# Delta solver of a hybrid encoder block: scratch by direction and head, loads by ranges of rows, side transfers on Pool's queue

## Chip, cores and metric

One core of one Trainium2 chip runs the kernel. The metric is device time in microseconds of one execution; before, the median of three runs is 1564.22 us. A core has TensorE (PE, matmuls), VectorE (DVE), ScalarE (ACT), GpSimd (POOL) and SyncE (SP); transfers are issued by an engine's queue and carried by 16 shared DMA engines.

## The reference, cut to what matters

One layer of an encoder over 256 tokens and 2048 channels, and a final norm. The first projection feeds a gated delta mixer in both directions (8 heads of 128 channels, chunks of 64 tokens) and a dilated window attention; the output projection and a convolutional gated feed-forward follow. The change touches the triangular solve of the delta mixer:

```python
    a_mat = jnp.where(strict, jnp.einsum("bhnik,bhnjk->bhnij", k_beta, k) * gamma, 0.0)
    t_mat = a_mat + jnp.eye(c, dtype=jnp.float32)
    u = lax.linalg.triangular_solve(t_mat, v * beta[..., None], left_side=True,
                                    lower=True, unit_diagonal=True)
    w = lax.linalg.triangular_solve(t_mat, k_beta * jnp.exp(cum_g)[..., None], left_side=True,
                                    lower=True, unit_diagonal=True)
```

There are 8 heads x 4 chunks x 2 directions = 64 triangular matrices of 64 x 64. The kernel inverts them once and multiplies by the inverse.

## The kernel before

**Main stream.** All projections are one list of items. An item is half of a 1 MB weight block (a slab of 1024 rows by 256 columns, one of two column halves): ACT rounds it to float32r (`hi`, line 262), DVE makes the rest (`lo`, line 263), and TensorE multiplies both with the transposed input `xcat` (lines 313 and 316). Weight blocks go round four buffers (`raws`, NR = 4). `refill` (line 248) issues the next block on SP as soon as, in program order, the block four earlier has been split; on the chip SP waits at that instruction for the split to be done. Items are split LA = 3 ahead of their matmuls.

**Side work.** Everything else is written as generators. `pump` advances them by a step after each item within a budget of vector and scalar time, so the order of instructions on each engine is fixed when the program is built, and each engine follows its own order, held only by data and by the reuse of tiles.

**Delta mixer, first part.** For each head, `g_conv` convolves q, k and v into a record; `g_gates` writes the cumulated decays to `cg_d` and loads them back for all partitions into `gam` (line 584, one load for each head on SP), where POOL adds the mask (line 592) and ACT takes the exponential (line 601). `g_gram` (line 733) makes the strictly triangular blocks `at` (the reversed direction with reversed columns) and writes them to the DRAM scratch `a_d` (line 774, POOL), the record to `rec_d`; gates of the output go to `z_d`.

**Solver.** `g_solve` (line 823) starts when all of these are written. Its tiles W (the inverses), tm (products) and Bt (the matrices) reuse the memory of the first part. Partitions are problems: `dir*64 + (s^dir)*32 + q*8 + h`, where s is the column parity of the inverse; so each matrix lies in two partitions. Bt is loaded in three ranges of rows (0 to 8 by SP, 8 to 24 and 24 to 64 by POOL), 16 loads each, of 8 partitions a load (line 850). Then 63 steps j run between the items, two DVE instructions each (lines 858 and 859): row j of Bt times column j of W, added to W. ACT reverses the backward half into tm (line 864), and 32 transfers write the inverses to `u_d` (line 874, half on SP and half on POOL; heads 0 and 1 first).

**Recurrence.** `g_steps` (line 923) takes over the solver's memory: zz and oo lie where W was, UB1 mostly where tm was, rr and UB0 where Bt was. DVE clears UB0 and POOL clears UB1 (line 938). SP copies four small scales, loads the inverses of the first two heads into UB0 (`load_u`, line 944), the records into rr (`load_r`, line 951), and, after WAIT_FIRST = 8 steps of the pump, the next pair's inverses and the gates zz (line 972). Four steps for each pair of heads follow, with the matmul by the inverse at line 998. `g_tail` norms and gates the outputs; POOL takes a power in it (line 894).

Of the kernel before, what the change touches and what calls it, by code (L numbers as in the profile page):

```python
# [4 lines left out]
F32 = mybir.dt.float32  # L5
# [24 lines left out]
WAIT_SOLVE = 6  # L30
TWO_PI = 2.0 * np.pi

# columns of the constant array
# [49 lines left out]
def block_kernel(tc, A, out, dbg=None):  # L83
# [17 lines left out]
    def aview(t, off, dims):  # L101
        """A view of an SBUF or PSUM tile with free dims given as [step, count]."""
        return bass.AP(tensor=t.tensor, offset=t.offset + off, ap=[list(t.ap[0])] + [list(d) for d in dims])
# [7 lines left out]
    # ------------------------------------------------------------ persistent tiles  # L111
# [39 lines left out]
    a_d = dram.tile([H, 4, P, 64], F32, name="a_d")  # L151
    u_d = dram.tile([H, 2, 4, 64, 64], F32, name="u_d")
    h_d = dram.tile([T, D], F32, name="h_d")

    # ------------------------------------------------------------ side work
# [9 lines left out]
    def pump(bv, ba=None):  # L165
        """Advance each piece of side work by one step, within the vector and scalar engines' time."""
        ba = bv if ba is None else ba
        state["v"] = min(state["v"] + bv, bv)
        state["a"] = min(state["a"] + ba, ba)
        for t in list(gens):  # L170
            if state["v"] <= 0 or state["a"] <= 0:
                break
            while True:
                try:
                    c = next(t[2])
                except StopIteration:
                    gens.remove(t)
                    break
                more = False
                if not isinstance(c, tuple):  # L180
                    c = (c, 0)
                elif len(c) == 3:
                    more = True
                state["v"] -= c[0]
                state["a"] -= c[1]
                if not more or state["v"] <= 0:
                    break
# [42 lines left out]
    # ------------------------------------------------------------ main stream  # L230
# [36 lines left out]
    def run_items(upto=None):  # L267
        """Emit the matmuls of all items listed so far."""
# [31 lines left out]
    def cm_block(ch, j, done, width=P):  # L300
        """Channel-major product of one block of columns: acc = [w.T xh + wl.T xh | w.T xl]."""
# [27 lines left out]
    def evac(out_ap, acc, n=P, perm=None):  # L329
        """out = acc[:, :256] + acc[:, 256:]."""  # L330
# [9 lines left out]
    def natural(ap):  # L340
        """Destination in token order for a source in class order."""
        return ap.rearrange("p (m c) -> p c m", c=4)

    # ------------------------------------------------------------ loads of constants, first norm
# [4 lines left out]
    # the small weights pass through the tiles that later hold the rotary tables  # L349
# [17 lines left out]
    # list of the first projection's items  # L367
# [7 lines left out]
    def v_slab(c0, done):  # L375
        """Token-major product of 256 columns, in class order of the tokens."""
# [41 lines left out]
    # sums of squares, scaled rows, transposes; the gate columns' product follows the transposes  # L418
# [68 lines left out]
    # ------------------------------------------------------------ side: small weights, gates, rotary tables  # L487
# [19 lines left out]
    def ab_write(fn, dst, src):  # L507
        """Chunk order 0,3,2,1 of the 64-token chunks."""
# [4 lines left out]
    def g_gates(graw, gg_, gpool):  # L513
# [18 lines left out]
        # sigmoid(x) = exp(min(x, 0)) / (1 + exp(-|x|))  # L532
# [3 lines left out]
        # log1p(e) = 2 z (1 + z^2/3 + z^4/5 + ...), z = e / (2 + e)  # L536
# [17 lines left out]
        # slot q: (tile, orientation) = (A,FB) (B,FB) (B,BF) (A,BF)  # L554
# [27 lines left out]
        # decay matrices of all heads: exp(cg_i - cg_j) inside the triangles  # L582
        for h in range(H):
            nc.sync.dma_start(gam[h], bass.AP(tensor=cg_d.tensor, offset=cg_d.offset + h * 512, ap=[[0, P], [1, 512]]))
# [3 lines left out]
        # ex: 0 -cg, 1 exp(cg), 2 -exp(cg), 3 exp(tot-cg), 4 exp(total of lower), 5 exp(total of upper), 6 cg  # L588
# [21 lines left out]
    # ------------------------------------------------------------ delta heads: convolution, Gram blocks  # L610
# [9 lines left out]
    for t in recs.free:  # L620
        for hf in range(2):
            # the blocks of different chunks
            G.memset(aview(t[hf * 64 : hf * 64 + 64], 1024 + hf * 64, [[P, 4], [1, 64]]), 0.0)
# [6 lines left out]
    # more buffers for the convolutions, gone before the attention's  # L630
# [12 lines left out]
    # a record holds, per tile of two chunks, the columns k0 q0 q1 k1 (64 each), then k by tokens, v by tokens, and the  # L643
    # products of q and k with the tokens of q in the order 1, 0 of the chunks
    def qk_write(fn, r, c0, src):
        """Tile 0 has the chunks 0 and 3, tile 1 the chunks 2 and 1."""
# [20 lines left out]
    def g_conv(which, h, pad):  # L667
# [37 lines left out]
        if which < 2:  # L705
# [10 lines left out]
            if which == 1:  # L716
                # 2: sqrt(ss + eps), 3: 1 / (ss + eps)
                G.tensor_tensor(ss[:, 2, :, h : h + 1], sc, poshalf[:, 0:2].rearrange("p (x o) -> p x o", o=1), op=ALU.pow)
                V.reciprocal(ss[:, 3, :, h : h + 1], sc)
            else:  # L720
                # 4: (128 (ss + eps))^(-1/2)
# [11 lines left out]
    def g_gram(h):  # L733
# [4 lines left out]
        # 0: beta / (ss+eps) per slot, 1: -that, 2: that * exp(tot - cg)  # L738
# [8 lines left out]
        # rows 0-63: k0 with k0 q0, rows 64-127: k1 with q1 k1  # L747
# [26 lines left out]
        nc.gpsimd.dma_start(a_d[h].rearrange("q p c -> p q c"), at)  # L774
# [29 lines left out]
    def z_pads():  # L804
        """From here on no pad of the extra pool is handed out."""
# [9 lines left out]
    # ------------------------------------------------------------ delta: triangular inverses and recurrence  # L815
    mx = {}

    def natural_31(fn, dst, src):
        """Token order for a source in chunk order 3,0,1,2."""
# [3 lines left out]
    def g_solve():  # L823
# [10 lines left out]
        # partition = dir*64 + (s^dir)*32 + q*8 + h, columns 2m+s of the inverse; bwd problems with rows and columns reversed  # L834
# [3 lines left out]
        for r0, r1 in ((0, 8), (8, 24), (24, 64)):  # L838
            for d in range(2):
                for s in range(2):  # L840
                    for o in range(2):
                        hf = o ^ d
                        p0 = d * 64 + (s ^ d) * 32 + o * 16
                        for i in range(2):
                            q = o * 2 + i
                            # the reversed rows leave out the columns below the diagonal; the others come in one piece
                            row, sj, c0 = (63 - r0, -64, r0) if d else (r0, 64, 0)
                            base = a_d.offset + (q * P + hf * 64 + row) * 64 + c0
                            src = bass.AP(tensor=a_d.tensor, offset=base, ap=[[4 * P * 64, 8], [sj, r1 - r0], [1, 64 - c0]])
                            (nc.gpsimd if r0 else nc.sync).dma_start(Bt[p0 + i * 8 : p0 + i * 8 + 8, r0:r1, c0:], src)  # L850
        for _ in range(WAIT_SOLVE):
            yield 0
        for j in range(63):
            m, r = j // 2 + 1, 63 - j
# [10 lines left out]
        for h0, h1 in ((0, 2), (2, H)):  # L865
            for d in range(2):
                for s in range(2):
                    for q in range(4):
                        hf = (q // 2) ^ d
                        p0 = d * 64 + (s ^ d) * 32 + q * 8  # L870
                        src = W[p0 + h0 : p0 + h1] if d == 0 else wr[p0 + h0 : p0 + h1]
                        dst = bass.AP(tensor=u_d.tensor, offset=u_d.offset + ((h0 * 2 + hf) * 4 + q) * 4096 + (s ^ d) * 64,
                                      ap=[[8 * 4096, h1 - h0], [128, 32], [1, 64]])
                        (nc.sync if q % 2 else nc.gpsimd).dma_start(dst, src)
# [5 lines left out]
    def g_tail(g0, o_t, z_t, jk):  # L880
        """Gated RMS norm of the heads from g0 on."""
# [41 lines left out]
    def g_steps():  # L923
        gt, tp = pool("steps", side="left")
        NG = 2
        # what is needed first lies where the solver's last transfers do not read
# [13 lines left out]
        def load_u(g0):  # L940
            t = UB[(g0 // NG) % 2]
            for hf in range(2):
                for e in range(NG):
                    nc.sync.dma_start(t[hf * 64 : hf * 64 + 64, e, :, hf * 64 : hf * 64 + 64],
                                        u_d[g0 + e, hf].rearrange("q c r -> c q r"))

        def load_r(g0, part):
            if g0 < H:
                cs = (slice(0, 1024), slice(1024, 1536))[part]
                for e in range(NG):  # L950
                    nc.sync.dma_start(rr[e][:, cs], rec_d[g0 + e, :, cs])

        # the outputs' tokens are held in the order 1, 0 of the chunks of a tile, and so are their scales
# [9 lines left out]
        for g0 in range(0, H, NG):  # L963
# [7 lines left out]
            for e in range(NG):  # L971
                nc.sync.dma_start(z_t[e], z_d[g0 + e])
# [84 lines left out]
    # ------------------------------------------------------------ dilated attention  # L1057
# [9 lines left out]
    def g_tables():  # L1067
        # rotary tables: angle = pos * inv_freq, reduced to [-pi, pi] with exact products
# [43 lines left out]
    def v_hook(g, pr, acc):  # L1112
        # wait for the readers of the former pair
# [94 lines left out]
    # ------------------------------------------------------------ output projection items  # L1208
    go, op = None, None

    def tm_group(w, k0, nk, c0, acc_of, act, first, last, done):
        """Token-major product of k-tiles k0.. with 512 columns."""
# [91 lines left out]
    # ------------------------------------------------------------ feed-forward items  # L1304
    # the first columns take the first half of the rows of all four blocks before the second half
# [22 lines left out]
    # the last rows of the last columns: the first 128 tokens, then the others  # L1328
# [87 lines left out]
    # ------------------------------------------------------------ down projection, final norm  # L1416
# [72 lines left out]
```

## Time and profile before

| | |
|---|---|
| times of three runs, us | 1560.75, 1564.22, 1568.68 |
| span of the profiled execution, us | 1562.7 |
| TensorE busy | 1523.4 us, 97% |
| VectorE, ScalarE, GpSimd busy | 71%, 54%, 8% |
| DMA moved | 300.63 MB, 192 GB/s over the span |

The profile is of one execution, from the first instruction to the last; its span is 1.5 us under the median of the runs. Busy time of TensorE is that of pipelined matmuls, whose ends are modelled. A granted clock below 1 means that TensorE ran, for part of the stretch, at the lower of its two levels. [...]

### The profile page before, as it was taken

How to read it: one execution, taken by the hardware profiler on the slowest of the kernel's cores; microseconds unless marked ns; L12 is line 12 of the kernel's file. 1: busy time of each engine (PE TensorE's matmuls, PEld its weight loads, DVE VectorE, ACT ScalarE, POOL GpSimd, SP SyncE). 2: the span in 40 equal slices, each digit the busy share in tenths (PEclk: the TensorE clock that was granted, in tenths of full speed). 3: DMA queues.
4: the chain of work that ended last, by engine and by line, in shares of the span. 5: the costliest groups of instructions: out<-in, count | busy, mean ns of one | idle time of the engine just before them, and what ended most of it. 6: DMA issues, size and time to landing. Idle time of an engine off the chain costs nothing.

```text
span 1562.7 us, 23126 instructions
## 1 busy us (share of the span) xinstructions
PE 1523.4 (97%) x8827; PEld 1326.9 (85%) x8827; DVE 1102.3 (71%) x1872; ACT 847.5 (54%) x1518; POOL 132.5 (8%) x189
## 2 busy tenths in 40 slices
PE   7999999899998999999999999999999999999997
PEld 6878888798997898899788888888888888888886
DVE  5878986879864676776557777777777777455453
ACT  5588774555544555654446555555555555344342
POOL 3153344000020000000000000000000000000000
PEclk9999999899999999999999999999999999999999
DMA  9656789755658645655665565656555556666652
GB/s 254 216 173 222 220 265 186 223 163 161 191 147 227 199 136 164 207 162 175 216 216 194 170 206 172 197 181 194 184 186 191 184 193 231 202 210 212 196 188 81
DMA packets 253569, 300.63 MB, mean 192 GB/s; under 512 B 16645, under 2 KB 214454, under 8 KB 253010
## 3 DMA queue, kind: packets, MB, share of 16 engines
q1 hardware_dynamic: 246802, 279.51, 57.6%
q0 software_dynamic: 6224, 19.05, 4.3%
q8 instruction: 69, 1.13, 0.3%
q10 hardware_dynamic: 432, 0.59, 0.1%
q14 instruction: 42, 0.34, 0.1%
HBM read 285.41 MB, written 13.65 MB: 191 GB/s over the span
## 4 chain that ended last, share of the span: by engine, by line
PE 92%; DMA 3%; issue 1%; ACT 1%; DVE 1%; POOL 0%; SPq 0%; POOLq 0%; ACTq 0%; DVEq 0%
PE bank L313 38%; PE bank L316 19%; PE bank L1224 7%; PE bank L1226 7%; PE bank L1225 7%; PE bank L391 3%; PE bank L392 3%; PE bank L393 3%; DMA raw<-in_w_in_dram 3%; PE bank L982 1%; PE bank L1028 1%; PE bank L1023 1%; DMA xt<-in_x_dram 0%; PE bank L1198 0%; PE bank L1179 0%
## 5 line engine op out<-in xcount | busy, mean ns | idle before, releaser
L313 PE MATMUL bank<-xcat,hi 128*128 128x512 f32 x2688 | 952.2, 399 | 18.6 <-DVE qk L338 15.2
L263 DVE TENSOR_TENSOR lo<-raw,hi 128x1024 fp32r<-128x1024 f32 x504 | 619.0, 1229 | 361.0 <-ACT hi L262 357.2
L262 ACT ACTIVATE hi<-raw 128x1024 fp32r<-128x1024 f32 x504 | 533.0, 1059 | 546.0 <-PE bank L313 211.6
L316 PE MATMUL bank<-xcat,lo 128*128 128x256 f32 x2688 | 730.1, 282 | 0.0
L313 PEld LDWEIGHTS bank<-xcat,hi 128*128 128x128 f32 x2688 | 499.0, 189 | 126.9 <-DVE qk L338 16.3
L316 PEld LDWEIGHTS bank<-xcat,lo 128*128 128x128 f32 x2688 | 506.8, 189 | 13.4
L1224 PE MATMUL bank<-hi,gth 128*128 128x512 f32 x336 | 130.7, 389 | 0.0
L1226 PE MATMUL bank<-hi,gtl 128*128 128x512 f32 x336 | 130.7, 389 | 0.0
L1225 PE MATMUL bank<-lo,gth 128*128 128x512 f32 x336 | 130.7, 389 | 0.0
L391 PE MATMUL bank<-hi,xcat 128*128 128x256 f32 x384 | 108.6, 283 | 0.0
L393 PE MATMUL bank<-hi,xcat 128*128 128x256 f32 x384 | 106.5, 277 | 0.0
L392 PE MATMUL bank<-lo,xcat 128*128 128x256 f32 x384 | 106.4, 277 | 0.0
L1392 DVE SCALAR_TENSOR_TENSOR fy<-fpad,cwf,fy 128x256 f32<-128x256 f32 x176 | 84.8, 482 | 3.1
L1225 PEld LDWEIGHTS bank<-lo,gth 128*128 128x128 f32 x336 | 63.1, 188 | 13.2
L1226 PEld LDWEIGHTS bank<-hi,gtl 128*128 128x128 f32 x336 | 63.1, 188 | 13.1
L1224 PEld LDWEIGHTS bank<-hi,gth 128*128 128x128 f32 x336 | 63.1, 188 | 12.9
L391 PEld LDWEIGHTS bank<-hi,xcat 128*128 128x128 f32 x384 | 72.1, 188 | 0.5
L393 PEld LDWEIGHTS bank<-hi,xcat 128*128 128x128 f32 x384 | 72.4, 189 | 0.0
L392 PEld LDWEIGHTS bank<-lo,xcat 128*128 128x128 f32 x384 | 72.2, 188 | 0.1
L1224 PE MATMUL bank<-hi,mxh 128*128 128x512 f32 x128 | 51.4, 401 | 0.3 <-DVE hs L1262 0.3
L1226 PE MATMUL bank<-hi,mxl 128*128 128x512 f32 x128 | 50.6, 395 | 0.0
L1225 PE MATMUL bank<-lo,mxh 128*128 128x512 f32 x128 | 50.6, 395 | 0.0
(288 smaller groups left out, 1333.6 us busy)
## 6 DMA issues: line engine op xcount, KB each, us to landing
raw<-in_w_in_dram SPq DMA_DIRECT2D x104, 1024.0 KB
raw<-in_w_ffn_in_dram SPq DMA_DIRECT2D x88, 1024.0 KB
raw<-in_w_ffn_out_dram SPq DMA_DIRECT2D x44, 1024.0 KB
raw<-in_w_out_dram SPq DMA_DIRECT2D x14, 1024.0 KB
rec_d<-rec POOLq DMA_DIRECT2D x8, 768.0 KB, 5.3
rr<-rec_d SPq DMA_DIRECT2D x8, 512.0 KB
xt<-in_x_dram SPq DMA_DIRECT2D x4, 512.0 KB
gam<-cg_d SPq DMA_DIRECT2D x8, 256.0 KB
```

Of the source, the lines that this page charges most:

```text
L262: ACT(hi, src, AF.Copy)
L263: V.tensor_sub(lo, src, hi.bitcast(F32))
L313: mm(acc[:, :512], lhsT=hi[:, kk, :], rhs=xcat[:, k, :], start=k == 0, stop=k == KT - 1)
L316: mm(acc[:, :T], lhsT=lo[:, kk, :], rhs=xcat[:, k, :T], start=False, stop=False)
L391: mm(o, lhsT=xh, rhs=hi[:, kk, :], start=k == 0 and t == 0, stop=False, skip_group_check=True)
L392: mm(o, lhsT=xh, rhs=lo[:, kk, :], start=False, stop=False, skip_group_check=True)
L393: mm(o, lhsT=xl, rhs=hi[:, kk, :], start=False, stop=k == KT - 1, skip_group_check=True)
L982: mm(p1[:, e * T + hf * P : e * T + (hf + 1) * P], lhsT=rr[e][:, X * T + hf * P : X * T + (hf + 1) * P], rhs=SS[e][:, o ^ hf, :], start=Tr ...
L1224: mm(a[t], lhsT=xh, rhs=hi[:, kk, :], start=st, stop=False)
L1225: mm(a[t], lhsT=xh, rhs=lo[:, kk, :], start=False, stop=False)
L1226: mm(a[t], lhsT=xl, rhs=hi[:, kk, :], start=False, stop=sp_)
L1392: stt(y, pad[:, d : d + T], cwf[:, d, b : b + 1], y, op0=ALU.mult, op1=ALU.add)
```

## The change

Both scratch tensors are laid out by direction, head, chunk: `a_d` and `u_d` are `[2, H, 4, 64, 64]`. `g_gram` writes a head's blocks with four transfers in place of one. Bt gets the partition order `dir*64 + copy*32 + h*4 + q`, so that a load covers 64 partitions (forward; the source is read twice by a step of zero) or 32 (backward, whole rows, in reversed order). The rows come in four ranges; the loads of the last two stand at steps j = 6 and j = 16 of the solver's loop. All of Bt's loads are on POOL. The inverses are written with 8 transfers in place of 32, all on POOL. `load_u` uses eight transfers for a pair of heads in place of four. The loads of gam, UB, zz and, from the second pair of heads on, rr move from SP to POOL. Comments are left out of the file. The core of the diff:

```diff
+ROWS = ((0, 8), (8, 24), (24, 44), (44, 64))
...
-    a_d = dram.tile([H, 4, P, 64], F32, name="a_d")
-    u_d = dram.tile([H, 2, 4, 64, 64], F32, name="u_d")
+    a_d = dram.tile([2, H, 4, 64, 64], F32, name="a_d")
+    u_d = dram.tile([2, H, 4, 64, 64], F32, name="u_d")
...
-            nc.sync.dma_start(gam[h], bass.AP(tensor=cg_d.tensor, offset=cg_d.offset + h * 512, ap=[[0, P], [1, 512]]))
+            nc.gpsimd.dma_start(gam[h], bass.AP(tensor=cg_d.tensor, offset=cg_d.offset + h * 512, ap=[[0, P], [1, 512]]))
...
-        nc.gpsimd.dma_start(a_d[h].rearrange("q p c -> p q c"), at)
+
+        for o in range(2):
+            for hf in range(2):
+                d = o ^ hf
+                base = a_d.offset + ((d * H + h) * 4 + 2 * o) * 4096
+                dst = bass.AP(tensor=a_d.tensor, offset=base, ap=[[64, 64], [4096, 2], [1, 64]])
+                nc.gpsimd.dma_start(dst, at[hf * 64 : hf * 64 + 64, 2 * o : 2 * o + 2, :])
...
-        for r0, r1 in ((0, 8), (8, 24), (24, 64)):
-            for d in range(2):
-                for s in range(2):
-                    for o in range(2):
-                        hf = o ^ d
-                        p0 = d * 64 + (s ^ d) * 32 + o * 16
-                        for i in range(2):
-                            q = o * 2 + i
-                            # the reversed rows leave out the columns below the diagonal; the others come in one piece
-                            row, sj, c0 = (63 - r0, -64, r0) if d else (r0, 64, 0)
-                            base = a_d.offset + (q * P + hf * 64 + row) * 64 + c0
-                            src = bass.AP(tensor=a_d.tensor, offset=base, ap=[[4 * P * 64, 8], [sj, r1 - r0], [1, 64 - c0]])
-                            (nc.gpsimd if r0 else nc.sync).dma_start(Bt[p0 + i * 8 : p0 + i * 8 + 8, r0:r1, c0:], src)
+
+        def load_rows(r0, r1):
+            src = bass.AP(tensor=a_d.tensor, offset=a_d.offset + r0 * 64, ap=[[0, 2], [4096, 32], [1, (r1 - r0) * 64]])
+            nc.gpsimd.dma_start(Bt[0:64, r0:r1, :].rearrange("p r c -> p (r c)"), src)
+            for s in range(2):
+                src = bass.AP(tensor=a_d.tensor, offset=a_d.offset + 32 * 4096 + (63 - r0) * 64,
+                              ap=[[4096, 32], [-64, r1 - r0], [1, 64]])
+                nc.gpsimd.dma_start(Bt[64 + s * 32 : 96 + s * 32, r0:r1, :], src)
+
+        for r0, r1 in ROWS[:2]:
+            load_rows(r0, r1)
         for _ in range(WAIT_SOLVE):
             yield 0
         for j in range(63):
+            for r0, r1 in ROWS[2:]:
+                if j == r0 // 2 - 6:
+                    load_rows(r0, r1)
...
-                    for q in range(4):
-                        hf = (q // 2) ^ d
-                        p0 = d * 64 + (s ^ d) * 32 + q * 8
-                        src = W[p0 + h0 : p0 + h1] if d == 0 else wr[p0 + h0 : p0 + h1]
-                        dst = bass.AP(tensor=u_d.tensor, offset=u_d.offset + ((h0 * 2 + hf) * 4 + q) * 4096 + (s ^ d) * 64,
-                                      ap=[[8 * 4096, h1 - h0], [128, 32], [1, 64]])
-                        (nc.sync if q % 2 else nc.gpsimd).dma_start(dst, src)
+                    p0 = d * 64 + s * 32
+                    src = (wr if d else W)[p0 + h0 * 4 : p0 + h1 * 4]
+                    dst = bass.AP(tensor=u_d.tensor, offset=u_d.offset + (d * H + h0) * 4 * 4096 + s * 64,
+                                  ap=[[4096, (h1 - h0) * 4], [128, 32], [1, 64]])
+                    nc.gpsimd.dma_start(dst, src)
...
-                    nc.sync.dma_start(t[hf * 64 : hf * 64 + 64, e, :, hf * 64 : hf * 64 + 64],
-                                        u_d[g0 + e, hf].rearrange("q c r -> c q r"))
+                    for o in range(2):
+                        src = u_d[o ^ hf, g0 + e, 2 * o : 2 * o + 2].rearrange("q c r -> c q r")
+                        nc.gpsimd.dma_start(t[hf * 64 : hf * 64 + 64, e, 2 * o : 2 * o + 2, hf * 64 : hf * 64 + 64], src)
...
-                    nc.sync.dma_start(rr[e][:, cs], rec_d[g0 + e, :, cs])
-
-        # the outputs' tokens are held in the order 1, 0 of the chunks of a tile, and so are their scales
+                    (nc.gpsimd if g0 else nc.sync).dma_start(rr[e][:, cs], rec_d[g0 + e, :, cs])
...
-                nc.sync.dma_start(z_t[e], z_d[g0 + e])
+                nc.gpsimd.dma_start(z_t[e], z_d[g0 + e])
```

## Rows read from the trace of the kernel before

**Rows 1.** The page: span, and busy time with instruction count of two engines.

```profile
span 1562.7 us, 23126 instructions
...
PE 1523.4 (97%) x8827; PEld 1326.9 (85%) x8827; DVE 1102.3 (71%) x1872; ACT 847.5 (54%) x1518; POOL 132.5 (8%) x189
```

**Rows 2.** TensorE's instructions in order of time (start, duration; idle before and releaser).

```profile
280.31 0.79 PE L313 MATMUL bank<-xcat,hi 128*128 128x512 f32 x1 [7.42 <-DVE qk L338]
...
489.84 0.70 PE L998 MATMUL bank<-rr,UB 128*128 128x128 f32 x4
497.44 0.80 PE L313 MATMUL bank<-xcat,hi 128*128 128x512 f32 x1 [6.90 <-DVE qk L338]
```

**Rows 3.** Windows: stretch, busy time by engine, granted clock, DMA share, GB/s.

```profile
280.30:286.30 6.00, 5.99 (x19) 5.15 (x20) 5.53 (x9) 1.48 (x3) 0.00 (x0) 0.53 0.67 203
286.30:292.30 6.00, 6.00 (x36) 5.23 (x35) 5.45 (x10) 4.08 (x8) 0.00 (x0) 1.00 0.68 217
...
497.40:501.40 4.00, 3.96 (x13) 3.44 (x14) 3.93 (x7) 2.98 (x8) 0.00 (x0) 0.56 0.82 219
```

**Rows 4.** The chain of waits that ended last: start, duration, what.

```profile
251.46 26.04 DMA raw<-in_w_in_dram
...
836.03 0.47 PE bank L313 x2
841.64 0.47 PE bank L313 x2
```

**Rows 5.** SP's queue in order of time: start, duration from first to last issue.

```profile
63.95 5.18 SPq L584 DMA_DIRECT2D gam<-cg_d  x8
...
227.45 2.37 SPq L253 DMA_DIRECT2D raw<-in_w_in_dram  x2
236.64 5.99 SPq L850 DMA_DIRECT2D Bt<-a_d  x16
...
451.50 3.15 SPq L253 DMA_DIRECT2D raw<-in_w_in_dram  x2
455.89 2.96 SPq L874 DMA_DIRECT2D u_d<-W  x4
461.87 1.64 SPq L874 DMA_DIRECT2D u_d<-tm  x4
...
474.81 0.83 SPq L253 DMA_DIRECT2D raw<-in_w_in_dram  x1
...
483.90 2.82 SPq L951 DMA_DIRECT2D rr<-rec_d  x4
```

**Rows 6.** DMA queues from 243 to 275, then 275 to 280: packets, MB, share.

```profile
q1 hardware_dynamic: 4194, 4.11, 81.2%
q0 software_dynamic: 865, 1.28, 29.5%
...
q1 hardware_dynamic: 1714, 1.73, 108.0%
```

**Rows 7.** POOL's instructions in order of time around both ends of the solver.

```profile
236.99 10.54 POOL L850 DMA_DIRECT2D Bt<-a_d  x19 [2.59 <-issue]
...
456.46 0.67 POOL L874 DMA_DIRECT2D u_d<-W  x1 [190.41 <-DVE W L859]
...
464.74 2.68 POOL L874 DMA_DIRECT2D u_d<-W  x4
...
478.00 0.96 POOL L938 MEMSET UB<- 128x1024 f32 x1 [7.55 <-DMA u_d<-tm]
```

**Rows 8.** ACT's instructions in order of time: the first reader of gam there.

```profile
82.46 1.27 ACT L601 ACTIVATE gam<-gam,ex 128x128 f32<-128x128 f32 x4
```

**Rows 9.** DMA issues: queue, count, KB each, median us to landing.

```profile
u_d<-W POOLq DMA_DIRECT2D x4, 48.0 KB, 7.2
...
u_d<-W POOLq DMA_DIRECT2D x4, 16.0 KB, 3.3
```

## The prediction

> **What bounds the kernel now.** I read the page first: TensorE is busy for 1523.4 of 1562.7 us [rows 1], so the kernel is a stream of matmuls, and only idle or slowed time of that engine can be won. The order of its instructions in time shows two long holes in the middle: 7.42 us ahead of 280.31, and 6.90 us ahead of 497.44 [rows 2]. The windows behind each hole show a second loss: the granted clock is 0.53 for 6 us (19 matmuls, against 36 in the next 6 us at 1.00) and 0.56 for 4 us [rows 3]. This is the 1.2 GHz level after an idle spell, then 2.4 GHz again. At full clock the same work takes (1 - 0.53) x 6.0 = 2.8 us and (1 - 0.56) x 4.0 = 1.8 us less. So the first hole costs 7.4 + 2.8 = 10.2 us, the second 6.9 + 1.8 = 8.7 us, together 18.9 us. The rest of the idle time, some 25 us of 39, lies at the start, at the end and in small pieces, where the diff has nothing, or work off the chain.
>
> Why the holes are there: the chain of waits names the landing of a weight block. One raw block of 1 MB feeds two items, and the stream eats one in 5.6 us (841.64 - 836.03) [rows 4]. The block issued at 251.46 took 26.04 us to land [rows 4], and TensorE stood for 7.42 of them; so 18.6 us from issue to landing would have cost nothing. That is the slack of four raw buffers and of the items split ahead.
>
> The timeline of SP's queue says why the blocks were late. Before the first hole SP issued two raw blocks by 229.8, then none until 242.6: it stood in the solver's sixteen first loads (236.64 for 5.99 us, and ahead of them a wait for its tile's former use) [rows 5]. Before the second hole it issued none from 454.65 to 474.81, held by the sixteen writes of the inverse (from 455.89 on), one at 474.81, and then scales, UB and rr until 486.72 [rows 5]. That is 20.2 us, 3.6 blocks' worth, and then 11 us more.
>
> There is a second cause for the first hole: the blocks that were issued moved slowly. From 243 to 275 SP's queue moved 4.11 MB in 81.2% of 16 engines (101 engine-ns per KB), while Pool's Bt loads moved 1.28 MB in 29.5% (118 per KB); from 275 to 280, alone, SP's queue took 50 per KB [rows 6]. Something in the Bt loads made every packet take twice as long. They go to 8 partitions at a time, which I suspect, but no row separates that from the many short pieces.
>
> **The change, part by part.**
>
> *SP loses the Bt loads, the u_d writes, UB, later rr, z and gam.* In the two places that count, SP keeps only the four small copies of scales and the four rr loads of the first pair (2.82 us) [rows 5]. Nothing that SP keeps there waits for the solver's writes: rr lies where Bt was, which no write reads. Raw blocks are then issued as buffers come free. For the second hole that alone is worth 8.7 us. For the first it returns the 13 us between 229.8 and 242.6, more than two blocks, against a lateness of 7.4 us. So both holes should close if the transfers themselves don't get worse.
>
> *The Bt loads.* 48 loads become 12: per range of rows one for the forward half (64 partitions, one long run each) and two of 32 partitions for the reversed half, now whole rows of 256 bytes. The bytes grow from 1.8 to 2.1 MB, the short pieces stay at about 4100 but each is longer. The last two ranges are placed at the solver's steps 6 and 16, but this moves only their place in Pool's order: Pool has no instruction between the Bt loads and the first u_d write at 456.46 (idle 190.41 us before it) [rows 7], and the loads read nothing that the steps write. So I expect all twelve right after one another, from about 237. At the 118 engine-ns per KB of before, 2.1 MB are 247 engine-us, 15.5 us of all sixteen. Raw blocks need 50 x 1024 ns = 51 engine-us each, 3.2 of every 5.6 us. Bounds: if raw packets keep their 50 ns, nothing is lost; if all of the 15.5 us goes ahead of a raw block, it lands 15.5 + 3.2 = 18.7 us after issue, which is just the slack of 18.6; if the packets slow to 101 ns as before for 32 us, the deficit of before returns without SP's 13 us. I take 0, since two of the three bounds lie there; the other end is the whole 10.2 us.
>
> The Trainium skill (DMA: Bandwidth & Descriptors, Rules for kernel authors) says that an access whose outermost dimension has few counts, such as a leading zero-step broadcast, confines a transfer to that many engines. The forward loads now have such a source (zero step, count two); By that rule the sum would be between 18.9 us (each load on engines of its own) and 7.4 us (all on the same two); no load of before has such a source, so its trace neither agrees nor disagrees.
>
> *The a_d writes.* Eight become 32, 24 more issues on Pool at about 0.55 us (the mean of the nineteen Bt issues, 10.54 us) [rows 7]: 13 us more on an engine that is busy for 8% [rows 1], before the solver, spread over eight heads. Cost 0; with the cover gone (the last head's four writes ahead of the first Bt load) the loads start 1.6 us later.
>
> *The gam loads* go from SP (5.18 us of its queue [rows 5]) to Pool. They now stand on Pool behind a wait for the landing of cg_d, and Pool's small powers and the mask additions stand behind them. ACT's first use of gam is at 82.46 [rows 8], 13 us after SP had issued the last load (69.1); eight issues at 0.55 us are 4.4 us. I take 0; the bounds are 0 and some 2 us.
>
> *The u_d writes and UB.* 32 writes become 8, of 64 and 192 KB; all on Pool. 16 UB loads become 32, eight for each pair of heads. Here Pool's order matters. Behind the eight writes stands the memset of the second UB tile, which lies in tm and waits for the writes that read it; before, it ran at 478.00 after 7.55 us of idling [rows 7]. Behind the memset now stand the first eight UB loads, which SP issued before, and for them waits TensorE's first step (L998, 489.84 [rows 2]), with the whole matmul stream behind it. When do the writes land? Low: the last is issued at about 467 (461.9, when tm is copied [rows 5], and six issues of, by my estimate from the 0.67 us of one before, up to 0.9 us) and lands after the 7.2 us of a 48 KB write [rows 9], at 474. Middle: the same 4096 pieces as before, done as before at 478. High: Pool's queue wrote its half of the large pieces from 464.7 [rows 7] to about 477.5, 13 us for 1536; at that rate its 3584 pieces after 461.9 take 30 us, until 492. From there 0.96 us memset, eight issues at 0.67 and the 3.3 us landing of a small write [rows 9] are 9.7 us. UB is there at 484, 488 or 502, against 489.84. Cost 0, 0 or 11.9 + 1.8 for the clock = 13.7 us. I take the middle, 0, with 2 us to spare. (Times are those of before; all behind 280 moves 10 us forward together.)
>
> *rr and z of later pairs* go to Pool and wait there for their last readers, as they did on SP; behind them on Pool stand only the power of the gated norm and the next loads, which have a pair's time, some 50 us. Cost 0.
>
> **Sum.** The span loses 10.2 + 8.7 = 18.9: 1543.8. The median of the runs shown, 1564.22, is 1.5 us above the span; so 1545.3 for the time.
>
> **The rivals.**
> 1. *Both holes close*: 1545.3. Its own range is 1542 to 1549, for pieces of 1 to 3 us left over and the spread of runs.
> 2. *TensorE waits for UB in place of the second hole.* For it: Pool alone now issues writes, memset and loads in one order, and there are 2 us to spare. Against: larger writes over more partitions may go faster. Halfway between middle and high (485), UB lands at 494.7: 4.9 + 1.8 = 6.7, so 1552; at the high end 1559.
> 3. *The first hole stays, by the forward loads.* Their source steps twice over the same 32 blocks, so it has an outermost count of two. If they rest on two engines each, and on the same two, an engine that moves 1.73 MB / 5 us / 16 = 21.6 KB per us [rows 6] has 512 KB of them, 24.3 us, and 64 KB of a raw block, 3.0 us: 27.3 us to landing, 8.7 over the slack, and 2.8 for the clock, 11.5 in all: 1556.8. On different pairs, the largest load is 160 KB, 7.6 + 3.0 us, and nothing is lost. Before's slowness returning in full gives nearly the same, 1555.5.
> 4. *It does not do what it says*: the shared transfer engines, not SP's order, starve the stream in both places: 1564.
> 5. *Slower.* One mechanism at one place: raw blocks, which were held back while the inverse was written, now run beside the writes and halve Pool's rate. 3584 pieces take 60 us, until 522; UB lands at 531.7, TensorE stands for 41.9 us and 1.8: 1545.3 + 43.7 = 1589. It decides from where that wait passes 17 us, that is when the writes end after 497. Against it: between 462 and 478 the engines were far from full.
>
> **How the numbers follow.** Chances: 0.60, 0.14, 0.12, 0.07 and 0.07. I predict the first, 1545. For the range, the low end is the first rival's with some spread, 1541; the high end takes in the second and third with their upper bounds, 1560, and leaves the last two out. About 0.5%, 7.8 us, is what a measurement can tell here: faster means below 1556.4. The first case, nearly all of the second (0.12) and half of the third (0.06) lie there: 0.78. The others of these and the fourth, 0.15, are the same; slower 0.07.
>
> **What the profile would show.** Right: no idle of TensorE above 3 us between 100 and 700, a granted clock of 1.00 around 270 and 490; raw issues of SP no further apart than about 12 us in both places; twelve Bt loads on Pool within some 15 us. Right or wrong on UB: whether L998 idles, and when the second UB memset runs. Wrong: ACT waiting for raw blocks for several us around 250 to 280 as before, or L998 released by a UB load. A reversed wait on gam would show as ACT idle at about 82.

## The result and the profile after

The changed kernel takes 1555.09 us (median of 6 runs, 1552.45 to 1558.9), the kernel before 1563.61 in runs beside it. The ratio is 0.9943, 95% interval 0.9928 to 0.9958: a gain of 0.6%, where 1.2% were forecast. The span went from 1562.7 to 1552.9 us [rows 1]. The page after, span and busy time:

```profile
span 1552.9 us, 23123 instructions
...
PE 1522.1 (98%) x8827; PEld 1326.1 (85%) x8827; DVE 1102.1 (71%) x1872; ACT 848.3 (55%) x1518; POOL 163.4 (11%) x245
```

TensorE's instructions in order of time, the ones with idle time ahead of them around the two holes, and the first use of UB (line numbers are 1 to 7 higher than before, so L1005 answers to L998):

```profile
269.32 0.80 PE L314 MATMUL bank<-xcat,hi 128*128 128x512 f32 x1 [7.86 <-DVE qk L339]
...
489.10 0.61 PE L1005 MATMUL bank<-rr,UB 128*128 128x128 f32 x4
```

Against [rows 2] the second hole is gone: no idle time is shown between 465 and 505, and L1005 starts without a wait. The first hole is still there, 7.86 us in place of 7.42. The window behind it:

```profile
269.30:275.30 6.00, 5.98 (x25) 5.20 (x26) 5.86 (x12) 3.17 (x7) 0.00 (x0) 0.72 0.66 208
```

The granted clock is 0.72 for 6 us, a loss of (1 - 0.72) x 6.0 = 1.7 us, against 2.8 before [rows 3]. So the first hole costs 9.6 us instead of 10.2, the second 0 instead of 8.7. Together that is 9.3 us; the spans differ by 9.8.

The chain of waits names the same releaser as in [rows 4], a raw block:

```profile
241.78 24.73 DMA raw<-in_w_in_dram
```

SP's queue in order of time, around the gates and at the end of the solver:

```profile
63.17 45.61 SPq L254 DMA_DIRECT2D raw<-in_w_in_dram  x8
...
440.17 25.74 SPq L254 DMA_DIRECT2D raw<-in_w_in_dram  x4
465.96 2.54 SPq L963 DMA_DIRECT2D ex<-ex  x1
...
473.28 3.10 SPq L958 DMA_DIRECT2D rr<-rec_d  x4
476.48 43.68 SPq L254 DMA_DIRECT2D raw<-in_w_in_dram  x8
```

Where SP had held raw blocks back for 20 us [rows 5], side transfers now stop it for 10.6 us (465.9 to 476.5). It stands ahead by then: the block issued at 465.54 was held for 11.5 us by the split that frees its buffer, not by a side transfer.

Ahead of the first hole SP has no side transfer left, and yet it issues no raw block between 231.08 and 239.85:

```profile
228.73 2.35 SPq L254 DMA_DIRECT2D raw<-in_w_in_dram  x2
...
239.85 2.30 SPq L254 DMA_DIRECT2D raw<-in_w_in_dram  x2
```

That gap of 8.8 us is a wait for DVE by the view of waits: a split (`lo`) ends at 239.82, and SP issues at 239.85. POOL in the same places:

```profile
63.86 4.31 POOL L585 DMA_DIRECT2D gam<-cg_d  x8 [1.74 <-issue]
...
70.70 1.59 POOL L593 TENSOR_TENSOR gam<-gam,cst 128x512 f32<-128x512 f32 x1 [1.55 <-DMA gam<-cg_d]
...
239.39 0.72 POOL L848 DMA_DIRECT2D Bt<-a_d  x1 [3.73 <-PE bank L314]
...
257.99 0.68 POOL L852 DMA_DIRECT2D Bt<-a_d  x1 [8.97 <-DMA Bt<-a_d]
...
475.05 0.96 POOL L944 MEMSET UB<- 128x1024 f32 x1 [9.07 <-DMA u_d<-tm]
475.95 4.73 POOL L952 DMA_DIRECT2D UB<-u_d  x8
```

All twelve Bt loads go out between 239.39 and 258.7, though the last six stand at steps 6 and 16 of the solver. POOL stops on the way for the landing of its own earlier loads, 8.97 us ahead of the last one. The writes of the inverse have landed by 475.05 (478.00 before [rows 7]).

Now the Bt loads themselves; the issues with their landing times (loads of 320 and 256 KB are forward, those of 160 and 64 KB reversed, 128 KB are one forward and two reversed):

```profile
Bt<-a_d POOLq DMA_DIRECT2D x2, 320.0 KB, 21.4
Bt<-a_d POOLq DMA_DIRECT2D x4, 160.0 KB, 21.0
...
Bt<-a_d POOLq DMA_DIRECT2D x3, 128.0 KB, 17.2
...
Bt<-a_d POOLq DMA_DIRECT2D x1, 256.0 KB, 16.5
Bt<-a_d POOLq DMA_DIRECT2D x2, 64.0 KB, 7.1
```

and the DMA queues from 239 to 267 (packets by size; for each queue packets, MB, share of 16 engines):

```profile
DMA packets 5534, 5.40 MB, mean 193 GB/s; under 512 B 1731, under 2 KB 5059, under 8 KB 5533
...
q1 hardware_dynamic: 3383, 3.41, 62.5%
q0 software_dynamic: 2150, 1.97, 41.3%
```

SP's queue (q1) takes 0.625 x 16 x 28 us / 3.41 MB = 82 engine-ns per KB (the time of its packets, summed over the 16 engines), less than the 101 of before but far from the 50 that it takes alone [rows 6]. The raw block issued at 241.78 is late for that. Its slack was 24.73 - 7.86 = 16.9 us.

### The profile page after: what moved, and what is told of

It reads as the page before. It is cut to its first block, busy times and chain, and to the rows that moved or that the text cites. A ratio compares the mean times of both kernels' runs of the same rounds, so it can differ in the third digit from the quotient of the medians.

```text
span 1552.9 us, 23123 instructions
## 1 busy us (share of the span) xinstructions
PE 1522.1 (98%) x8827; PEld 1326.1 (85%) x8827; DVE 1102.1 (71%) x1872; ACT 848.3 (55%) x1518; POOL 163.4 (11%) x245
## 4 chain that ended last, share of the span: by engine, by line
PE 93%; DMA 2%; issue 1%; DVE 1%; ACT 1%; POOL 0%; POOLq 0%; SPq 0%; ACTq 0%; DVEq 0%
PE bank L314 38%; PE bank L317 19%; PE bank L1231 7%; PE bank L1232 7%; PE bank L1233 7%; PE bank L392 3%; PE bank L394 3%; PE bank L393 3%; DMA raw<-in_w_in_dram 2%; PE bank L989 1%; PE bank L1035 1%; PE bank L1030 1%; ACT kb L759 1%; DVE lo L264 0%; PE bank L1205 0%
```

## The experiments

Three theories of the remaining hole were on record before the first runs. **A**: the forward loads rest on few engines, since their source has an outermost count of two, and raw blocks wait for these. **B**: the reversed rows' 4096 short pieces slow every packet. **C**: all twelve loads at once are too much, in whatever shape. Spans and idle times are of the profiled execution; ratios are to the kernel before on the same chip.

**No load of Bt at all.**

```diff
         def load_rows(r0, r1):
...
+            G.memset(Bt[:, r0:r1, :], 0.0)
```

> This kernel leaves out the loads of the matrices: Bt is cleared by Pool in place of them, so the inverses are wrong. If the Bt loads are what is left of the first hole, as all theories here say, TensorE has no idle piece above 3 us between 100 and 700, and the time is about 1545 (1555.1 less 7.9 us of idle and 1.7 us of low clock). If the hole has another cause (the writes just ahead, SP, the splits), it stays near 7.9 us and the time near 1555.

1544.01 us, ratio 0.9867 (0.985 to 0.9883), span 1542.0. No idle piece of TensorE is left in the stretch from 240 to 330. So the Bt loads are what remained of the hole, and the forecast's sum (1545.3 with both holes closed) was the right size.

**Two forward loads of 32 partitions, no zero step.**

```diff
-            src = bass.AP(..., ap=[[0, 2], [4096, 32], [1, (r1 - r0) * 64]])
-            nc.gpsimd.dma_start(Bt[0:64, r0:r1, :].rearrange("p r c -> p (r c)"), src)
+            for s in range(2):
+                src = bass.AP(..., ap=[[4096, 32], [1, (r1 - r0) * 64]])
+                nc.gpsimd.dma_start(Bt[s * 32 : s * 32 + 32, r0:r1, :].rearrange("p r c -> p (r c)"), src)
```

> The forward rows are loaded by two transfers of 32 partitions each instead of one whose source steps twice by zero. Theory A (the forward loads rest on few engines, and a raw block lands when its slowest engine is done): the forward loads land in well under 10 us instead of 16 to 21, the 24.7 us of the late raw block falls under 17, the hole closes, time about 1546. Theory B (the reversed rows' 4096 short pieces slow every packet): landing of the reversed loads stays about 20 us, the hole stays at 6 us or more, time about 1554. Theory C (all twelve loads at once are too much, in whatever shape): as B.

1546.97 us, ratio 0.9882 (0.9868 to 0.9897), span 1545.4. This kernel beats both. TensorE's largest idle piece there, the issues of Bt, and the queues from 239 to 267:

```profile
263.05 0.50 PE L314 MATMUL bank<-xcat,hi 128*128 128x512 f32 x1 [0.98 <-DVE qk L339]
```

```profile
Bt<-a_d POOLq DMA_DIRECT2D x8, 160.0 KB, 9.1
...
Bt<-a_d POOLq DMA_DIRECT2D x4, 128.0 KB, 7.7
...
Bt<-a_d POOLq DMA_DIRECT2D x4, 64.0 KB, 4.3
```

```profile
DMA packets 5318, 6.69 MB, mean 239 GB/s; under 512 B 337, under 2 KB 4805, under 8 KB 5317
...
q1 hardware_dynamic: 4548, 4.58, 62.2%
q0 software_dynamic: 769, 2.10, 32.9%
```

The same bytes land in about half the time, the reversed loads too, which were not touched (their median over all sizes is 8.4 in place of 17.6 us); raw packets take 0.622 x 448 / 4.58 = 61 engine-ns per KB. That is in the main what theory A forecast, though no view shows how many engines carry a load. C falls: twelve (now sixteen) loads at once make no hole above 1 us in this shape. The time is 3 us above that without any load, where the intervals of the two ratios overlap.

**Reversed rows as one long run.**

```diff
-                src = bass.AP(..., offset=a_d.offset + 32 * 4096 + (63 - r0) * 64, ap=[[4096, 32], [-64, r1 - r0], [1, 64]])
+                src = bass.AP(..., offset=a_d.offset + 32 * 4096 + r0 * 64, ap=[[4096, 32], [1, (r1 - r0) * 64]])
```

> The reversed rows are loaded in forward order, as one long run for each partition (the same bytes, no short pieces), so the backward inverses are wrong; the forward loads are as changed. Theory A: the hole stays at 6 us or more, the forward loads still land after 16 to 21 us. Theory B: the hole closes, packets of the raw blocks go back from 82 to about 50 engine-ns per KB, span about 1543. Theory C: the hole stays, perhaps smaller.

Span 1552.0, one time of 1553.79. The hole stays:

```profile
267.93 0.80 PE L314 MATMUL bank<-xcat,hi 128*128 128x512 f32 x1 [6.47 <-DVE qk L339]
```

The loads land as in the changed kernel (20.9 us for 160 KB), and 1807 packets under 512 bytes are still there though no reversed row is cut any more. Theory B falls. The 1.4 us by which the hole is shorter are no more than executions differ by: with all Bt loads as changed it is 6.51 us in a run below.

**The last two ranges really held until steps 6 and 16.**

```diff
                 if j == r0 // 2 - 6:
+                    G.tensor_copy(tk, W[:, 0, j : j + 1])
                     load_rows(r0, r1)
```

> Ahead of each of the last two ranges Pool copies one column of W that the step before has written, so that these loads really start at steps 6 and 16 and not with the others. Theory C: the first six loads (0.8 of 2.1 MB) no longer make a raw block late by more than its slack; the hole closes or is under 3 us, and no new one opens at the later two ranges; time about 1546. Theory A: the hole shrinks only as far as the load on one pair of engines does (192 of 512 KB if they share a pair, to nothing if not). Theory B: it shrinks, and a new hole may open after step 6.

1550.72 us, ratio 0.9903 (0.9888 to 0.9917), span 1546.9. POOL now waits for the solver, and the hole shrinks to 2.69 us, with no new one behind it:

```profile
256.62 0.32 POOL L862 COPY tk<-W 128x1 f32<-128x1 f32 x1 [13.17 <-DVE W L869]
...
283.76 0.54 POOL L862 COPY tk<-W 128x1 f32<-128x1 f32 x1 [24.64 <-DVE W L869]
```

```profile
264.63 0.50 PE L314 MATMUL bank<-xcat,hi 128*128 128x512 f32 x1 [2.69 <-DVE qk L339]
```

Without that copy nothing ties POOL to the steps, as the issue times of the changed kernel show. Two of the four forward loads at a time still make a hole, a smaller one. A hole under 3 us is also what theory C had forecast here, so this run does not part A from C; the two forward loads do. The slow loads were not repaired: the 256 KB forward load still landed after 17.2 us.

**Both repairs at once** (two forward loads, and the copy).

> Both repairs at once: two forward loads of 32 partitions each, and the last two ranges held until steps 6 and 16 by a copy of one column of W. If what the repaired forward loads left (1547.0 against 1544.0 without any load) is the amount that is under way at once, this comes to 1544 to 1545, with no idle piece above 1 us between 100 and 700. If it is the first six loads alone, it stays at 1546 to 1547.

1545.95 us, ratio 0.9873 (0.9846 to 0.99), no idle piece in the stretch from 240 to 330. Its interval overlaps that of the two forward loads alone, so the holding back adds nothing that these runs can tell.

**What in the forward loads is slow?** Four kernels change only the source's form, the first against the two forward loads above, the others against the changed kernel. In the first, the two loads of 32 partitions list their blocks in two groups:

```diff
-            src = bass.AP(..., ap=[[0, 2], [4096, 32], [1, (r1 - r0) * 64]])
+            for s in range(2):
+                src = bass.AP(..., ap=[[4096, 2], [8192, 16], [1, (r1 - r0) * 64]])
+                nc.gpsimd.dma_start(Bt[s * 32 : s * 32 + 32, r0:r1, :].rearrange("p r c -> p (r c)"), src)
```

> As the run with two forward loads of 32 partitions, but their sources list the 32 blocks as two groups of every second block (outermost count two, no zero step); the blocks reach other partitions than they should, so the forward inverses are wrong. Theory A1 (a small outermost count puts the load on few engines): forward loads land after 15 us or more again, the hole is back at 5 us or more, span above 1550. Theory A2 (the zero step itself, or one load over 64 partitions, is what is slow): landing stays at 4 to 9 us and the span at about 1545.

Neither came out. The span is 1545.8 and the hole stays away:

```profile
274.91 0.50 PE L314 MATMUL bank<-xcat,hi 128*128 128x512 f32 x1 [1.53 <-DVE qk L339]
```

But landing of the 160 KB loads went up to 14.0 us from 9.1, and 1879 packets under 512 bytes are back. In the second, the zero step moves inside:

```diff
-            ... ap=[[0, 2], [4096, 32], [1, (r1 - r0) * 64]]
+            ... ap=[[4096, 32], [0, 2], [1, (r1 - r0) * 64]]
```

> As changed, one forward load of 64 partitions with the zero step, but the 32 blocks are its outermost dimension and the two copies the inner one (so partitions get other blocks, and the forward inverses are wrong). Theory A1: outermost count 32, so the load spreads, lands in under 10 us, the hole closes, span about 1545. Theory A2: the hole stays at 6 us or more, span about 1552.

Span 1543.2, 320 KB landed in 10.6 us, 256 packets under 512 bytes, as A1 said. TensorE, then SP's queue from 239 to 267 and the reversed loads of 160 KB:

```profile
260.88 0.50 PE L314 MATMUL bank<-xcat,hi 128*128 128x512 f32 x1 [0.87 <-DVE qk L339]
```

```profile
q1 hardware_dynamic: 4790, 4.84, 63.4%
...
Bt<-a_d POOLq DMA_DIRECT2D x4, 160.0 KB, 10.5
```

The same 32 blocks are read twice, as in the changed kernel. But its two edits (outermost count, place of the zero step) are not apart yet; the last two do that.

```diff
-            ... ap=[[0, 2], [4096, 32], [1, (r1 - r0) * 64]]
+            ... ap=[[4096, 2], [8192, 32], [1, (r1 - r0) * 64]]
```

> The changed kernel with one number of the forward loads changed: the outermost count of two steps to the next block (4096) and not by zero, and the inner 32 take every second block, so one load of 64 partitions reads 64 different blocks (the forward inverses are wrong). If the outermost count of two is the cause, nothing changes: landing 16 to 21 us, some 1800 packets under 512 bytes while the loads run, hole 6 us or more, span about 1552. If reading the same bytes twice by a zero step is the cause: landing under 12 us, hole under 2 us, span about 1545.

and

```diff
-            ... ap=[[0, 2], [4096, 32], [1, (r1 - r0) * 64]]
+            ... ap=[[0, 16], [4096, 4], [1, (r1 - r0) * 64]]
```

> The changed kernel with the forward source [[0, 16], [4096, 4], ...]: an outermost zero step again, but with count sixteen (four blocks read sixteen times; the forward inverses are wrong). If a small outermost count is the cause: landing under 12 us, fewer than 500 packets under 512 bytes, no hole, span about 1544. If the outermost zero step is the cause: as changed, hole 6 us or more, span about 1552.

TensorE in the first, then its queues from 239 to 267:

```profile
269.66 0.79 PE L314 MATMUL bank<-xcat,hi 128*128 128x512 f32 x1 [9.16 <-DVE qk L339]
```

```profile
DMA packets 5399, 5.24 MB, mean 187 GB/s; under 512 B 1747, under 2 KB 4925, under 8 KB 5398
```

The same two of the second:

```profile
262.12 0.50 PE L314 MATMUL bank<-xcat,hi 128*128 128x512 f32 x1 [1.44 <-DVE qk L339]
```

```profile
DMA packets 5064, 6.51 MB, mean 232 GB/s; under 512 B 259, under 2 KB 4551, under 8 KB 5063
```

An outermost count of two without a zero step makes the hole, span 1554.3; an outermost zero step with count sixteen does not, span 1544.4. So in loads of 64 partitions the small outermost count is the cause, not the zero step or the repeated reading. The count alone is not enough: with two loads of 32 partitions it lengthened the landing, but made no hole above 1.53 us.

**SP gets half of the writes and all of UB back** (in the changed kernel).

```diff
-                    nc.gpsimd.dma_start(dst, src)
+                    (nc.sync if s else nc.gpsimd).dma_start(dst, src)
...
-                        nc.gpsimd.dma_start(t[hf * 64 : ...
+                        nc.sync.dma_start(t[hf * 64 : ...
```

> The changed kernel with half of the eight writes of the inverse and all UB loads back on SP. If SP's order made the second hole, SP stands behind the copy of tm again and behind the landing of the writes: the raw blocks near 470 come late and an idle piece of 2 to 7 us is back around 480 to 495; span 1555 to 1562. If the larger writes (8 in place of 32) closed it, there is still no idle piece there and the span stays near 1553.

Span 1555.6, and a second hole beside the first:

```profile
266.45 0.80 PE L314 MATMUL bank<-xcat,hi 128*128 128x512 f32 x1 [6.51 <-DVE qk L339]
...
490.60 0.79 PE L314 MATMUL bank<-xcat,hi 128*128 128x512 f32 x1 [2.94 <-DVE qk L339]
```

SP's order makes it: only the queue of these transfers differs from the changed kernel. It is less than half of the old one; that SP has 4 writes in place of 16 is the likely reason. The time of this one run, 1557.49, lies within the spread of the changed kernel's; the hole is what the trace shows.

**The kernel before, with all Bt loads on POOL.**

```diff
-                            (nc.gpsimd if r0 else nc.sync).dma_start(Bt[...
+                            nc.gpsimd.dma_start(Bt[...
```

> The kernel before with one edit: its sixteen first Bt loads are issued by Pool, so that SP issues none. The prediction held that SP's 13 us without a raw block made the block late and that giving them back closes the first hole: then the hole falls from 7.4 to under 2 us, span about 1553. If the loads of 8 partitions slow the raw packets whoever issues them, the hole stays at 5 us or more, span 1558 to 1564.

Span 1557.7. Both holes of this kernel:

```profile
287.09 0.50 PE L313 MATMUL bank<-xcat,hi 128*128 128x512 f32 x1 [1.84 <-DVE qk L338]
...
492.15 0.80 PE L313 MATMUL bank<-xcat,hi 128*128 128x512 f32 x1 [6.96 <-DVE qk L338]
```

The first falls from 7.42 to 1.84 us with the old loads of 8 partitions, 48 of them. The second is untouched. The span, expected at about 1553, is missed: the time is 1559.47 against 1561.59 in one run of the kernel before beside it, and two single runs don't settle such a difference.

The edit does not act on SP's order alone. SP's queue from 243 to 275, as in [rows 6]:

```profile
q1 hardware_dynamic: 5599, 5.65, 67.8%
```

Raw packets took 0.678 x 512 / 5.65 = 61 engine-ns per KB there, in place of 101. And SP issued two raw blocks by 232.3 and the next at 241.07: of the 13 us without a raw block, 8.8 are left.

**The kernel before, with all writes of the inverse and UB on POOL**, in their old shapes.

```diff
-                        (nc.sync if q % 2 else nc.gpsimd).dma_start(dst, src)
+                        nc.gpsimd.dma_start(dst, src)
...
-                    nc.sync.dma_start(t[hf * 64 : ...
+                    nc.gpsimd.dma_start(t[hf * 64 : ...
```

> The kernel before with one edit: all 32 writes of the inverse and the 16 UB loads are issued by Pool, in their old shapes. If SP's order alone made the second hole, it closes (no idle piece above 2 us between 450 and 520) and the first stays at 7 to 8 us: span about 1554. If Pool cannot finish 32 writes in time, TensorE waits for a UB load at its first use instead, for 2 to 12 us.

Span 1567.0. The hole by raw blocks is replaced by a wait for UB, at the place of the second rival:

```profile
496.39 1.20 PE L998 MATMUL bank<-rr,UB 128*128 128x128 f32 x4 [3.58 <-DMA UB<-u_d]
```

TensorE also waited 1.9 us for rr later (L1023), and the first hole was 8.05 us. The time is 1568.76 against 1561.59 in one run of the kernel before beside it; by how much it is longer, one run of each does not settle.

## Why the prediction failed, point by point

*What bounds the kernel, and what the holes are worth*: right. With the cause of both removed (no load of Bt) the time is 1544.0 against a forecast of 1545.3.

*SP loses its transfers*: right for the second hole. It closed in full, and comes back in part when SP gets work back. For the first hole the return was sized wrong: SP was to get 13 us back, more than two blocks, and got 4, less than the 7.4 us of idle; closing the hole needed faster raw packets as well. Without any side transfer it still issues nothing for 8.8 us (231.08 to 239.85), because it waits for a split to free a buffer. The same edit of queue in the kernel before takes 5.6 of the first hole's 7.4 us away, but the raw packets were faster in that run too (61 in place of 101 engine-ns per KB from 243 to 275). How the old first hole divides between SP's order and the slow packets stays open.

*The Bt loads*: this is the step that failed. I took a cost of 0 out of three bounds, since two of them lay there, and the loads cost 9.6 us. Two of the bounds were worked out with the price per KB of the old loads, as if their shape did not matter; that two of three agree is no evidence. The real loads made raw packets cost 82 engine-ns per KB, the third bound nearly. The second bound (18.7 us from issue to landing) was no 0 either: the slack turned out to be 16.9 us, not 18.6. What SP's order and the old loads had cost at this spot was taken away, and a new fault (the forward source's outermost count of two) put in its place with nearly the same price: 9.6 us against 10.2. That is why the profile looks as if the first hole had not been touched. It is the third rival, to which I gave 0.12: it gave 1556.8, and 1555.1 was measured. Its sum assumed that all forward loads share one pair of engines. On different pairs, it said, nothing is lost. Which engines carry them no view shows, so the near agreement does not confirm that sum. The loads of before have an outermost count too, of eight; the prediction leaves it out where it asks why they are slow, and no run here changes it.

The rule of the Trainium skill that stood against the change (DMA: Bandwidth & Descriptors, Rules for kernel authors: a small outermost count keeps a transfer to that many engines) agrees with the loads of 64 partitions: 7.86 and 9.16 us of hole with two, 1.44 with sixteen and 0.87 with 32. It deserved more than a rival of 0.12. What the rule gives as the mechanism, the number of engines, is not shown here. The mean busy share of the engines was 1.04 (62.5% + 41.3%) in the slow stretch, and it is a mean. A second mark of the count of two is 1731 to 1879 packets under 512 bytes from 239 to 267 in place of 256 to 337, in the runs that issue all loads in that stretch. Their number alone does not make the hole: with two loads of 32 partitions and the count of two there were 1879 and an idle piece of 1.53 us. Whether the number of engines decides, or the amount that a single load puts on each of them, stays open.

*That the last two ranges are not delayed by the steps*: right (239.39 to 258.7); I said some 15 us, it was 19.

*a_d, gam, rr and z*: cost 0, right. The first mask addition on POOL is at 70.70 in place of 70.83, and TensorE has no new idle piece there.

*The u_d writes and UB*: a cost of 0, as forecast, but two sizes were off and cancelled. The writes had landed at 475.05, between the low value (474) and the middle (478); the first UB loads took 6.3 us to land (the median of eight), where 3.3 was put. L1005 did not wait. The kernel before with the same queues but the old shapes waits 3.58 us at that place: there POOL's last write goes out at about 483, here at 466. So the fewer and larger writes are part of the gain, not only the move to POOL.

## What to carry to other kernels

Moving side transfers off the queue that feeds TensorE is worth the idle time that the queue's order makes. The timeline of that queue against the spacing of the weight blocks gives an upper bound before anything is built: part of a gap can be a wait for a buffer that stays, as 8.8 of 13 us did at the first hole. When the same change also reshapes the transfers, price the new shape by itself: look at the outermost count of both sides of each load first, and try a larger count there (sixteen and 32 closed the hole that two made). A transfer written into a loop of another engine's steps is not delayed by them, unless its own engine waits for something that the steps make.

## What was not expected of the hardware

A busy share near 1 says little about the work done: from 239 to 267 the engines moved 193 GB/s at a share of 1.04 in the changed kernel, and from 275 to 280 before they moved 345 GB/s at 1.08, with SP's queue alone [rows 6]. And slow transfers on one queue slow the others' packets on the way: with only the order of the forward source's dimensions changed (the zero step inside), the reversed loads of 160 KB landed in 10.5 in place of 21.0 us, and the raw blocks' packets took 0.634 x 448 / 4.84 = 59 in place of 82 engine-ns per KB.
